# Laying x and the result out in token order of the tiles, and finishing the last four tiles from their first complete half

## The chip, the cores and the metric

The kernel runs on one core of one Trainium2 chip. The metric is the device time of one execution in microseconds. Beside it stands the profile of one execution: its span goes from the first to the last instruction.

The engines are named as in the profile: PE (TensorE, matmuls), PEld (its weight loads), DVE (VectorE), ACT (ScalarE), POOL (GpSimd), SP (SyncE). SP computes nothing here; it issues most of the loads and stores. A name with a q, such as SPq, is the sequencer of an engine, and rows of DMA issues stand there.

## The reference, cut to what matters

One layer of a hybrid encoder, in float32, over 1024 tokens of width 1024 and a feed-forward width of 2816:

```
h = x + 0.5 * swiglu(rms_norm(x, ffn1_norm), w_gate1, w_up1, w_down1)
h = h + merged_attention(rms_norm(h, mix_norm)) @ w_out
h = h + 0.5 * swiglu(rms_norm(h, ffn2_norm), w_gate2, w_up2, w_down2)
return rms_norm(h, final_norm)
```

with `rms_norm(x, g) = x * rsqrt(mean(x * x) + 1e-6) * g` for each token. The merged attention joins a two-dimensional neighbourhood attention (a grid of 16 rows of 64 columns) and a windowed attention through two gates. The change touches the first line's x and the last line's norm.

## The kernel before, in words

**Tiles.** The 1024 tokens are worked on as eight tiles of 128. A tile isn't 128 tokens in a row: because of the grid attention, tile b takes the eight columns 8b to 8b+7 of each of the 16 grid rows. A token is a row of 1024 floats, 4 KB. So in the arrays x and out, a tile is 16 groups of 8 rows; a group is 32 KB in one piece, and the groups lie 64 rows, 256 KB, apart. The views `x2` and `out2` (L41, L42) say this, and each load or store of a tile goes through them. What the kernel puts away for itself, such as the residual `h_d`, it lays out tile by tile, so that a tile is 128 rows in one piece.

**The residual** lives in eight tiles `res(t)`: 0 to 3 in the buffers `fx`, 4 to 7 in the four quarters of `fa`.

**Float32 products.** Each factor is split in a high and a low part (`split`, L88: ACT copies the high part, DVE subtracts; the rows L89 and L90 of the profile), and each product takes three matmuls (`mm3`, L138; L141, L143, L145). The large products use a Strassen-like scheme of seven block products with the names P1 to P7.

**The start.** `load_x` (L587) loads the eight x tiles in SP's queue: tile 0, then the gain of the norm, tiles 1 to 3, the first two blocks of weights, tiles 4 to 7, two more blocks of weights. `transition` (L160) takes the tiles through the norm (`normed`, L112), the transpose on PE (`turned`, L134) and `to_strassen` (L189), which splits them into right-hand factors and copies the transposed halves (L204, L205). The products of the first half feed-forward begin when the first four tiles are through. In `normed`, ACT squares a tile and sums the squares (L119), POOL turns the sum into a factor (L122, L123), and DVE scales (L125). Each engine works its instructions in the order of its own queue.

**The down projections** are made by the class `Down`. Its list `seq` holds 77 pairs of a block product and one of 11 blocks, in the order P2, P1, P5, P6, P3, P7, P4. `run` (L526) goes through all but the last five and prepares the factors up to seven entries ahead, in a ring of seven slots; a slot is free when PE is through with the entry that had it. `evict` (L518, the DVE rows at L523) adds a finished PSUM bank, times 0.5, to a half tile of the residual. P7 completes the high half (columns 512 to 1023) of tiles 4 to 7; P4 completes their low half and is the last product. The last five entries, all of P4, are done tile by tile: `tail(j)` (L545) multiplies them for tile 4+j and evicts that tile, so that the tiles end one after another. For the residual of the first half feed-forward x is loaded once more (L572, in `down_ffn`, L566); the second one loads `h_d` with the same line.

**The end.** The loop at L1186 runs the second half feed-forward's down projection. `finish` (L1180) takes tile t through the final norm in two halves and stores each half, 128 rows of 2 KB, through SP (L1184). Tiles 0 to 3 are finished while the P4 entries run; tiles 4 to 7 behind their `tail`. `normed` with `parts=2` squares both halves, and POOL adds the two sums (L121), adds EPS (L122) and raises to the power -0.5 (L123); then DVE scales both halves, and each is stored.

**Order.** Engines are synchronised by semaphores that a tile framework sets; it also places each engine's instructions, so the order on an engine can differ from that of the source. Buffers named xs, raw, ws come from pools of 2, 4 and 8; who takes a buffer waits until its last user is done, a store from it included.

Of the kernel before, what the change touches and what calls it, by code (L numbers as in the profile page):

```python
# [10 lines left out]
F32 = mybir.dt.float32  # L11
F32R = mybir.dt.float32r
AF = mybir.ActivationFunctionType
ALU = mybir.AluOpType

P = 128
T = 1024
D = 1024
NC8 = D // P
NTT = T // P  # L20
# [4 lines left out]
ROWS = T // GW  # L25
NEG = -1.0e30
BIG = 1.0e38
EPS = 1e-6
# [8 lines left out]
def trunk_kernel(ctx, tc, x, n1, wg1, wu1, wd1, nm, win, rpb, sink, wa, wb, wo,  # L37
                 n2, wg2, wu2, wd2, nf, c_rope, c_mask_a, c_mask_b, out):
    nc = tc.nc

    x2 = x.rearrange("o (r b w) d -> (o b) r w d", b=NTT, w=8)  # L41
    out2 = out.rearrange("o (r b w) d -> (o b) r w d", b=NTT, w=8)  # L42

    const = ctx.enter_context(tc.tile_pool(name="const", bufs=1))
    main = ctx.enter_context(tc.tile_pool(name="main", bufs=1))
# [5 lines left out]
    def nm_(s):  # L51
        uid[0] += 1
        return f"{s}_{uid[0]}"
# [3 lines left out]
    nhalf = const.tile([P, 1], F32, name="nhalf")  # L57
# [11 lines left out]
    def new_ar(g, dt=F32R):  # L69
        ar[g] = main.tile([P, 4, 1024], dt, tag=f"ar{g}", bufs=1, name=nm_("ar"))  # L70
        return ar[g]
# [7 lines left out]
    def raw4():  # L79
        return main.tile([P, 1024], F32, tag="raw", bufs=4, name=nm_("raw"))  # L80

    def xs4():
        return main.tile([P, 1024], F32, tag="xs", bufs=2, name=nm_("xs"))
# [23 lines left out]
    def load_gain(g):  # L107
        gb = const.tile([P, 1152], F32, tag="gain", bufs=1, name=nm_("gain"))
        nc.sync.dma_start(gb[:, :D], g.partition_broadcast(P))
        return gb[:, :D]  # L110

    def normed(h, gb, xs=None, parts=1):  # L112

        xs = xs4() if xs is None else xs
        w = D // parts
        cols = [slice(i * w, (i + 1) * w) for i in range(parts)]
        st = const.tile([P, 4], F32, tag="st", bufs=4, name=nm_("st"))
        for i, c in enumerate(cols):
            nc.scalar.activation(xs[:, c], h[:, c], AF.Square, scale=D ** -0.5, accum_out=st[:, i:i + 1])  # L119
        if parts == 2:  # L120
            nc.gpsimd.tensor_tensor(st[:, 0:1], st[:, 0:1], st[:, 1:2], op=ALU.add)  # L121
        nc.gpsimd.tensor_scalar(st[:, 0:1], st[:, 0:1], EPS, None, op0=ALU.add)  # L122
        nc.gpsimd.tensor_tensor(st[:, 2:3], st[:, 0:1], nhalf, op=ALU.pow)  # L123
        for c in cols:
            nc.vector.scalar_tensor_tensor(out=xs[:, c], in0=h[:, c], scalar=st[:, 2:3], in1=gb[:, c],  # L125
                                           op0=ALU.mult, op1=ALU.mult)
        return xs
# [25 lines left out]
    def res(t):  # L153

        return fx[t] if t < 4 else fa[:, (t - 4) * 1024:(t - 3) * 1024]
# [435 lines left out]
    gain = load_gain(n1[0])  # L591
# [22 lines left out]
    gain = load_gain(nm[0])  # L614
# [458 lines left out]
    for n in range(1 << 30):  # L1073
# [14 lines left out]
        if n in (59, 60, 61):  # L1088
            c = (59, 60, 61).index(n)
# [10 lines left out]
    t = new_ar(2, F32)  # L1100
# [42 lines left out]
    for i, dc in enumerate(a_order):  # L1143
        r = nxt.pop(0)
# [11 lines left out]
        for n in range(2):  # L1156
            sl = slice(n * 512, (n + 1) * 512)
# [6 lines left out]
    gain = load_gain(n2[0])  # L1164
# [13 lines left out]
    gain = load_gain(nf)  # L1178

    def finish(t):  # L1180
        y = normed(res(t), gain, raw4() if t in (5, 7) else None, 2)
        for n in range(2):
            sl = slice(n * 512, (n + 1) * 512)
            nc.sync.dma_start(out2[t][:, :, sl], y[:, sl])  # L1184

    for n, _ in enumerate(down.run()):  # L1186
        if n in (2, 5, 8, 11):
            finish(n // 3)
    for t in range(4, NTT):
        down.tail(t - 4)  # L1190
        finish(t)


def _consts():
# [53 lines left out]
```

## Time and profile before

| what | us |
|---|---|
| median of 3 runs | 1960.69 |
| lowest and highest run | 1960.07, 1963.54 |
| the profiled execution, its own time | 1959.04 |
| its span | 1956.9 |
| PE busy in the span | 1923.9 |
| DVE busy | 1432.2 |
| ACT busy | 951.6 |
| POOL busy | 337.1 |

How to read what is quoted below. The page of the profile begins with the busy time of each engine and with lines of 40 digits, one for each fortieth of the span: the busy share in tenths. The table by stretches has one row for each stretch, `from:to`, its length, and then for PE, PEld, DVE, ACT and POOL the busy time and, in brackets, the number of instructions; behind these stand the clock granted to PE, the mean busy share of the 16 DMA engines, and the GB/s they moved. In the rows in order of time stand start, duration, engine, line, operation, what is written and read, and the count; in square brackets the idle time of the engine just before, and what ended it. Rows of one line's instructions give the shortest, the median and the longest duration in ns, and the first and the last start in us. Rows of groups give the total busy time in us and the mean of one instruction in ns. The end of a matmul is modelled.

### The profile page before, as it was taken

The numbers are of one execution on the slowest core, as the hardware profiler recorded it, in microseconds if no ns is written. First come the engines' busy times: TensorE is split into PE (matmuls) and PEld (weight loads), VectorE is DVE, ScalarE is ACT, GpSimd is POOL, SyncE is SP. The second block draws the span as 40 slices with busy tenths as digits, with TensorE's granted clock in tenths as the row PEclk, the third lists the DMA queues.
The fourth block names the chain that finished last, engine by engine and source line by source line (L and its number), as shares of the span: only waits on it lengthen the run. The fifth ranks groups of instructions, "written<-read, shape, count | busy, mean of one in ns | idle before, by whom it ended". The sixth has DMA issues, their size and how long they took to land. (4 is left out here: it accounts for less than half of the span.)

```text
span 1956.9 us, 25669 instructions
## 1 busy us (share of the span) xinstructions
PE 1923.9 (98%) x8968; PEld 1603.6 (82%) x8968; DVE 1432.2 (73%) x2503; ACT 951.6 (49%) x1846; POOL 337.1 (17%) x469
## 2 busy tenths in 40 slices
PE   6999999999999999999999999999999999999997
PEld 5888888888888888888888888878888888888886
DVE  7976566557967688678888857989666566569864
ACT  7433333334446543467787873366333333344452
POOL 1010001002500112211112135510101001005110
PEclk9999999999999999999999999999999999999999
DMA  8433323369233558663359565544523323492341
GB/s 212 145 114 103 118 87 108 119 219 281 82 119 129 170 176 261 207 180 92 97 141 190 180 228 210 178 140 146 151 86 108 119 92 104 147 358 90 119 145 49
DMA packets 234784, 293.45 MB, mean 150 GB/s; under 512 B 14208, under 2 KB 161024, under 8 KB 234656
## 3 DMA queue, kind: packets, MB, share of 16 engines
q1 hardware_dynamic: 206816, 206.24, 34.7%
q0 software_dynamic: 27840, 85.58, 13.2%
q8 instruction: 71, 1.16, 0.2%
q14 instruction: 57, 0.47, 0.1%
HBM read 205.16 MB, written 86.70 MB: 149 GB/s over the span
## 5 line engine op out<-in xcount | busy, mean ns | idle before, releaser
L141 PE MATMUL g<-ar,ws 128*128 128x512 f32 x1152 | 432.9, 395 | 2.3 <-ACT ar L89 1.6
L143 PE MATMUL g<-ar,ws 128*128 128x512 f32 x1152 | 426.6, 390 | 0.0
L145 PE MATMUL g<-ar,ws 128*128 128x512 f32 x1152 | 425.4, 390 | 0.2 <-DVE ws L90 0.2
L90 DVE TENSOR_TENSOR ws<-raw,ws 128x512 fp32r<-128x512 f32 (+1 forms) x329 | 235.7, 722 | 176.9 <-ACT ws L89 175.6
L89 ACT CAST ws<-raw 128x512 fp32r<-128x512 f32 (+1 forms) x331 | 209.4, 638 | 289.3 <-PE g L145 123.0
L143 PE MATMUL d<-ar,ws 128*128 128x512 f32 x712 | 271.9, 389 | 1.1 <-POOL ar L90 1.1
L141 PE MATMUL d<-ar,ws 128*128 128x512 f32 x712 | 272.3, 390 | 0.6 <-ACT ws L89 0.5
L145 PE MATMUL d<-ar,ws 128*128 128x512 f32 x712 | 271.8, 389 | 0.6 <-DVE ws L90 0.5
L145 PEld LDWEIGHTS g<-ar,ws 128*128 128x128 f32 x1152 | 216.2, 188 | 46.5 <-DVE ws L90 0.7
L143 PEld LDWEIGHTS g<-ar,ws 128*128 128x128 f32 x1152 | 216.2, 188 | 45.5 <-DVE ar L90 0.3
L141 PEld LDWEIGHTS g<-ar,ws 128*128 128x128 f32 x1152 | 211.1, 188 | 40.8 <-ACT ar L89 2.0
L141 PEld LDWEIGHTS d<-ar,ws 128*128 128x128 f32 x712 | 133.6, 188 | 29.1 <-ACT ws L89 1.5
L143 PEld LDWEIGHTS d<-ar,ws 128*128 128x128 f32 x712 | 133.6, 188 | 29.0 <-POOL ar L90 1.5
L145 PEld LDWEIGHTS d<-ar,ws 128*128 128x128 f32 x712 | 133.6, 188 | 28.8 <-DVE ws L90 1.0
L356 POOL DMA_DIRECT2D hid<-fx x96 | 51.8, 540 | 504.1 <-DVE fx L398 380.3
L90 DVE TENSOR_TENSOR ws<-ar,ws 128x512 fp32r<-128x512 f32 x114 | 109.1, 964 | 5.0 <-ACT ws L89 5.0
L89 ACT CAST ar<-raw 128x512 fp32r<-128x512 f32 (+1 forms) x83 | 56.0, 678 | 91.5 <-PE g L143 53.1
L90 DVE TENSOR_TENSOR ws<-fa,ws 128x512 fp32r<-128x512 f32 x76 | 52.5, 691 | 53.3 <-ACT ws L89 52.9
L141 PE MATMUL g<-ws,ws 128*128 128x512 f32 x232 | 91.0, 392 | 0.0
L145 PE MATMUL g<-ws,ws 128*128 128x512 f32 x232 | 90.4, 390 | 0.0
L143 PE MATMUL g<-ws,ws 128*128 128x512 f32 x232 | 90.3, 389 | 0.0
L1021 ACT ACTIVATE fa<-fa,nmx 128x385 f32<-128x385 f32 (+3 forms) x128 | 75.5, 591 | 27.2 <-DVE nmx L1018 26.6
(234 smaller groups left out, 3508.0 us busy)
## 6 DMA issues: line engine op xcount, KB each, us to landing
raw<-hid SPq DMA_DIRECT2D x70, 512.0 KB
hid<-fx POOLq DMA_DIRECT2D x96, 256.0 KB, 2.5
raw<-in_ffn_w_up_dram SPq DMA_DIRECT2D x32, 512.0 KB
ar<-in_ffn_w_down_dram SPq DMA_DIRECT2D x32, 512.0 KB
raw<-in_ffn_w_gate_dram SPq DMA_DIRECT2D x28, 512.0 KB
hid<-fa POOLq DMA_DIRECT2D x54, 256.0 KB, 2.6
raw<-in_w_in_dram SPq DMA_DIRECT2D x27, 512.0 KB
ar<-zs_d POOLq DMA_DIRECT2D x48, 256.0 KB, 5.0
```

What stands on the lines that cost most here:

```text
L89: nc.scalar.copy(dst_hi, src)
L90: (eng or nc.vector).tensor_tensor(dst_lo, src, f32v(dst_hi), op=ALU.subtract)
L141: nc.tensor.matmul(b, lhs[0], r[0], start=first, stop=False, **kw)
L143: nc.tensor.matmul(b, lhs[0], r[1], start=False, stop=False, **kw)
L145: nc.tensor.matmul(b, lhs[1], r[0], start=False, stop=last, **kw)
L356: nc.gpsimd.dma_start(hid[PRODUCTS.index(p), i], src)
L1021: nc.scalar.activation(pr, pr, AF.Exp, scale=-1.0, bias=nmx[:, s:s + 1], accum_out=ssum[:, s:s + 1])
```

## The change

The host hands x over with the tokens sorted by tile, and puts the rows of the result back into token order when the kernel is done; neither is in the device time. The views `x2` and `out2` are then plain: a tile is 128 rows of 4 KB in one piece. All loads of x (L588, L572) and all stores of the result go through the new views.

The finish of tiles 4 to 7 is taken apart. When the P7 evictions have completed the high half, four calls of `begin`, one behind each of four P4 entries, square that half on ACT, add EPS to its sum on POOL, and multiply the half by the gain on DVE. Behind the tail of a tile, `rest` squares the low half on ACT, adds the two sums and raises to the power on POOL. `scale` multiplies the low half by factor and gain on DVE and stores it through SP, and multiplies the high half by the factor on ACT and stores it through ACT's own queue. In the source, `scale` of a tile stands behind the tail of the next one.

In the built program PE's instructions and their order are unchanged. On DVE, the eviction of tile 4 is followed by the low-half scaling of tile 4, then come the eviction of tile 5, the scaling of tile 5, and so on. On ACT, each of the last four tiles has the low square, the high scaling and the DMA issue one behind the other. The four squares and the four multiplications of `begin` stand between the casts and subtractions of the last factors.

```diff
-    x2 = x.rearrange("o (r b w) d -> (o b) r w d", b=NTT, w=8)
-    out2 = out.rearrange("o (r b w) d -> (o b) r w d", b=NTT, w=8)
+    x2 = x.rearrange("o (b p) d -> (o b) p d", p=P)
+    out2 = out.rearrange("o (b p) d -> (o b) p d", p=P)
...
-            nc.sync.dma_start(out2[t][:, :, sl], y[:, sl])
+            nc.sync.dma_start(out2[t][:, sl], y[:, sl])
+
+
+    LO, HI = slice(0, 512), slice(512, 1024)
+    late = {}
+
+    def square(t, c, k):
+        y, st = late[t]
+        nc.scalar.activation(y[:, c], res(t)[:, c], AF.Square, scale=D ** -0.5, accum_out=st[:, k:k + 1])
+
+    def begin(t):
+        y, st = late[t] = raw4() if t in (5, 7) else xs4(), const.tile([P, 4], F32, tag="st", bufs=4, name=nm_("st"))
+        square(t, HI, 1)
+        nc.gpsimd.tensor_scalar(st[:, 1:2], st[:, 1:2], EPS, None, op0=ALU.add)
+        nc.vector.tensor_tensor(y[:, HI], res(t)[:, HI], gain[:, HI], op=ALU.mult)
+
+    def rest(t):
+        square(t, LO, 0)
+        st = late[t][1]
+        nc.gpsimd.tensor_tensor(st[:, 0:1], st[:, 0:1], st[:, 1:2], op=ALU.add)
+        nc.gpsimd.tensor_tensor(st[:, 2:3], st[:, 0:1], nhalf, op=ALU.pow)
+
+    def scale(t):
+        y, st = late[t]
+        nc.vector.scalar_tensor_tensor(out=y[:, LO], in0=res(t)[:, LO], scalar=st[:, 2:3], in1=gain[:, LO],
+                                       op0=ALU.mult, op1=ALU.mult)
+        nc.sync.dma_start(out2[t][:, LO], y[:, LO])
+        nc.scalar.activation(y[:, HI], y[:, HI], AF.Copy, scale=st[:, 2:3])
+        nc.scalar.dma_start(out2[t][:, HI], y[:, HI])
 
     for n, _ in enumerate(down.run()):
         if n in (2, 5, 8, 11):
             finish(n // 3)
+        if n in (12, 13, 14, 15):
+            begin(n - 8)
     for t in range(4, NTT):
         down.tail(t - 4)
-        finish(t)
+        rest(t)
+        if t > 4:
+            scale(t - 1)
+    scale(NTT - 1)
...
     data.update(_consts())
+    order = np.arange(T).reshape(ROWS, NTT, 8).transpose(1, 0, 2).reshape(-1)
+    data["x"] = np.asarray(data["x"])[:, order]
...
-    return r.results[0]["out_0_dram"]
+    out = np.empty_like(r.results[0]["out_0_dram"])
+    out[:, order] = r.results[0]["out_0_dram"]
+    return out
```

## The prediction

> **What bounds the kernel now.** I read the page first, then a table by stretches of the span, then the instructions in order of time at both ends. The profiled execution took 1959.04 us, its span 1956.9; the sum is made in that span. The median of the runs shown is 1960.69, so 1.65 above it, and a gain found in the span is taken off 1960.69.
>
> ```profile
> span 1956.9 us, 25669 instructions
> ...
> PE 1923.9 (98%) x8968; PEld 1603.6 (82%) x8968; DVE 1432.2 (73%) x2503; ACT 951.6 (49%) x1846; POOL 337.1 (17%) x469
> ...
> PE   6999999999999999999999999999999999999997
> ```
>
> ```profile
> 24.40:30.00 5.60, 5.17 (x26) 4.23 (x27) 5.60 (x9) 5.38 (x11) 1.49 (x3) 1.00 1.14 272
> 30.00:40.00 10.00, 9.93 (x53) 8.05 (x51) 10.00 (x16) 9.87 (x19) 1.71 (x4) 1.00 0.76 188
> 40.00:60.00 20.00, 19.91 (x92) 16.34 (x92) 19.28 (x32) 12.37 (x23) 1.32 (x2) 1.00 0.48 159
> ...
> 1900.00:1946.90 46.90, 46.85 (x206) 38.17 (x204) 23.75 (x38) 17.18 (x36) 3.91 (x12) 1.00 0.24 71
> ```
>
> TensorE (second column) is busy from its first real matmul to its last, 0.6 us of gaps in the first 36 and almost none later; only the first and the last slice of the page are below 9. So the time is three pieces: the start up to that first matmul (24.41 us, row below), a body of 1922.5, and a tail from the last matmul's end (1946.48 + 0.39 = 1946.87) to 1956.9, 10.0 us. The change adds no matmul and moves none, so it can pay only at the two ends.
>
> **The start: x laid out in token order.** Eight x tiles are loaded by L588, four before the first weights.
>
> ```profile
> 5.82 1.06 ACT L119 ACTIVATE xs<-fx 128x1024 f32<-128x1024 f32 x1 [3.81 <-DMA fx<-in_x_dram]
> ...
> 10.03 1.06 ACT L119 ACTIVATE xs<-fx 128x1024 f32<-128x1024 f32 x1 [3.06 <-DMA fx<-in_x_dram]
> ...
> 14.15 1.06 ACT L119 ACTIVATE xs<-fx 128x1024 f32<-128x1024 f32 x1 [0.80 <-DMA fx<-in_x_dram]
> ...
> 16.15 0.63 ACT L89 CAST ws<-raw 128x512 fp32r<-128x512 f32 x1
> ...
> 18.32 0.59 ACT L204 COPY fx<-d 128x512 f32<-128x512 f32 x1 [0.56 <-DVE ar L90]
> ...
> 24.41 0.50 PE L141 MATMUL g<-ar,ws 128*128 128x512 f32 x1 [1.63 <-ACT ar L89]
> ```
>
> ACT waits for each of the first four x tiles. After the fourth (14.15) it is busy nearly without a break until it releases TensorE at 24.41. So the start moves with the landing of the fourth tile. How fast is such a load? The next rows are stretches in which little but one kind of load moves (the last two columns are DMA share and GB/s): x tiles in 8 to 12, then two loads of h_d in contiguous rows, then one load of the rope table, an input like x but contiguous.
>
> ```profile
> 8.00:12.00 4.00, 1.97 (x8) 1.57 (x8) 1.24 (x1) 1.15 (x2) 0.65 (x2) 1.00 1.04 241
> ...
> 1112.50:1114.50 2.00, 2.00 (x13) 1.74 (x12) 1.95 (x9) 1.93 (x6) 0.38 (x1) 1.00 0.93 373
> 703.40:705.00 1.60, 1.60 (x9) 1.33 (x8) 1.60 (x4) 1.60 (x5) 0.00 (x0) 1.00 0.84 310
> ...
> L572 SPq DMA_DIRECT2D fx<-in_x_dram x4: 536/557/612, 414.0 to 454.3; - x4
> ...
> L572 SPq DMA_DIRECT2D fx<-h_d x4: 332/335/339, 1702.6 to 1742.1; - x4
> ```
>
> The x load keeps the DMA engines fully busy (1.04) at 241 GB/s; the same 512 KB in contiguous rows moves at 373 (share 0.93). Both go in rows of 4 KB, so packet size is not it; what differs is where the 128 rows lie (16 groups of 8 rows, 256 KB apart, against one run). The rope row says that it is not that x is an input: 310 at a share of 0.84 is again about 370 at full share. After the change x has h_d's layout. A tile of 524 KB takes 524/241 = 2.17 us before and 1.41 at 373, 0.77 less. Of the first four tiles three come back to back at the slow rate (2.3 us saved). The first starts on an idle queue and should save about half as much (0.4), and its issue is 0.56 - 0.34 = 0.22 us shorter. That makes 2.9 us for the fourth tile. ACT's following chain needs the first weights (16.15, 2.0 us behind the fourth square) and these were loaded behind the x tiles, so they come earlier by as much; tiles 4 to 7 come earlier by more. **I take 2.9 us off the start.** Bounds: 0 if the layout is not the cause, 3.9 at the rate of 412 that the fastest contiguous stretch shows, with the first tile at full saving.
>
> ```profile
> 1743.50:1745.00 1.50, 1.50 (x8) 1.23 (x8) 1.11 (x2) 0.31 (x1) 0.00 (x0) 1.00 1.03 412
> ```
>
> (524/412 = 1.27 us, 0.90 less a tile, four tiles 3.6, and the shorter issue.) The residual loads of x (L572, four tiles to each half) run below a full TensorE and count for nothing.
>
> The Trainium skill bears on this, in "DMA: Bandwidth & Descriptors", section "Latency and other measured facts": copies whose rows lie a large power of two apart slow down, but at a pitch of 512 KiB by only 3% (207 against 214 GB/s), and much at 2 MiB. By that rule a jump of 256 KB costs almost nothing, and the start would gain an estimated 0.3 us (3% of four loads). This case's rows, 241 against 373, speak for more.
>
> **The tail: what each part costs.** Rows of the last two tiles, in order of time:
>
> ```profile
> 1936.70 0.69 DVE L523 SCALAR_TENSOR_TENSOR fa<-g,fa 128x512 f32<-128x512 f32 x1 [7.08 <-PE g L145]
> ...
> 1944.79 0.68 DVE L523 SCALAR_TENSOR_TENSOR fa<-g,fa 128x512 f32<-128x512 f32 x1
> ...
> 1946.48 0.39 PE L145 MATMUL g<-ar 128*128 128x512 f32 x1
> ...
> 1947.50 1.42 DVE L125 SCALAR_TENSOR_TENSOR xs<-fa,st,gain 128x512 f32<-128x512 f32 x2 [2.02 <-POOL st L123]
> ...
> 1948.83 0.68 DVE L523 SCALAR_TENSOR_TENSOR fa<-g,fa 128x512 f32<-128x512 f32 x1
> 1949.55 0.63 ACT L119 ACTIVATE raw<-fa 128x512 f32<-128x512 f32 x1 [2.70 <-DVE fa L523]
> ...
> 1950.34 0.19 POOL L121 TENSOR_TENSOR st<-st 128x1 f32<-128x1 f32 x1 [2.88 <-ACT raw L119]
> 1950.62 0.22 POOL L122 TENSOR_SCALAR st<-st 128x1 f32<-128x1 f32 x1
> 1950.93 0.57 POOL L123 TENSOR_TENSOR st<-st,nhalf 128x1 f32<-128x1 f32 x1
> 1951.53 1.42 DVE L125 SCALAR_TENSOR_TENSOR raw<-fa,st,gain 128x512 f32<-128x512 f32 x2 [2.02 <-POOL st L123]
> 1952.31 1.20 SPq L1184 DMA_DIRECT2D out_dram<-raw  x2
> ```
>
> Step 1, the evictions. TensorE releases the first of these evictions at 1936.70 and ends the fourth tile at 1946.87, so it needs 3.39 us for a tile, but VectorE evicts one every 4.04 (1944.79 to 1948.83), because each eviction stands behind both scalings of the tile before, and these behind the whole chain eviction, square, POOL, scaling. The last eviction comes at 1948.83, though its bank was full at 1946.87. The source wants the scaling of tile t-1 behind the eviction of t, but the built kernel still places scale t ahead of eviction t+1. What cures it is that the chain is shorter: eviction to square 0.72, square to POOL 0.79, add 0.28, power 0.60, one scaling instead of two 0.71: 3.1 us, under 3.39. So the last eviction starts at 1946.90: **1.93 us** gained.
>
> Step 2, POOL. Adding EPS (L122) is done ahead: 1950.93 - 1950.62 = **0.31 us**. The last scaling may start 2.70 - 0.31 = 2.39 us behind the eviction, at 1949.29 instead of 1951.53.
>
> Step 3, two halves on two engines. VectorE scales the low half (store on SP at 1949.29 + 0.78 = 1950.07), ACT the high half, already multiplied with the gain; nearest row a 128x512 ACTIVATE at 0.63, at most 0.75, its store from ACT at about 1950.0. Before, the second store was issued 0.66 behind the first. What that is worth depends on the transfers:
>
> ```profile
> 1953.00:1954.00 1.00, 0.00 (x0) 0.00 (x0) 0.00 (x0) 0.00 (x0) 0.00 (x0) 0.50 0.45 88
> 1954.00:1955.00 1.00, 0.00 (x0) 0.00 (x0) 0.00 (x0) 0.00 (x0) 0.00 (x0) 0.50 1.00 320
> 1955.00:1956.00 1.00, 0.00 (x0) 0.00 (x0) 0.00 (x0) 0.00 (x0) 0.00 (x0) 0.50 0.32 117
> ```
>
> The 525 KB flow from about 1953.55 to 1955.3 without a gap: the second store queues behind the first, so its earlier issue gains nothing by itself. The Trainium skill says the same in "DMA: Bandwidth & Descriptors", section "Issuing engines are not separate DMA queues": two issuers share the 16 DMA engines, and a second one saves only issue time. The trace agrees (share 1.00 at 320 GB/s); by that rule alone this step would give 0, by the issue times 0.66.
>
> Step 4, the layout of out. Here too 16 groups become one run: the issue was 0.54 us (next row) and should be about 0.34 as for h_d, and 320 GB/s may rise towards 373, 0.2 us over 525 KB. I take **0.4 us** for steps 3 and 4 together, with 0 and 0.9 as bounds.
>
> ```profile
> L1184 SPq DMA_DIRECT2D out_dram<-raw x4: 538/538/539, 1944.2 to 1953.0; - x4
> ```
>
> Sum of the tail: 1.93 + 0.31 + 0.4 = **2.6 us** (2.2 to 3.1); the wait for the last store and the end of the program stay as they are.
>
> **What is moved into the body.** Ahead of the last five blocks VectorE gets four multiplications of about 0.69 and ACT three squares of 0.8 (to the POOL step behind them, as above; the fourth stood ahead of the end already before).
>
> ```profile
> 1919.76 0.62 ACT L89 CAST ws<-raw 128x512 fp32r<-128x512 f32 x1 [1.39 <-PE g L145]
> ...
> 1925.62 0.69 DVE L90 TENSOR_TENSOR ar<-raw,ar 128x512 fp32r<-128x512 f32 x1 [1.43 <-ACT ar L89]
> ...
> 1937.43 0.63 ACT L119 ACTIVATE xs<-fa 128x512 f32<-128x512 f32 x1 [8.61 <-DVE fa L523]
> ...
> 1902.50 1.20 SPq L1184 DMA_DIRECT2D out_dram<-xs  x2
> ```
>
> There ACT idles 1.4 us before each pair of casts, waiting for TensorE to free a slot, and 8.6 us at the end; seven slots are ready ahead of TensorE. Cost nothing. Without that cover it would be 2.5 us of ACT. The new wait there is ACT's, for tile 3's store before it reuses its buffer; behind it stand the casts, for which TensorE would wait. That store is issued at 1902.50 (last row), and the square that reuses the buffer comes behind casts of about 1919, so it has long landed.
>
> ACT's DMA issue is new. SP's costs 0.54, POOL's 0.54:
>
> ```profile
> L356 POOL DMA_DIRECT2D hid<-fx x96 | 51.8, 540 | 504.1 <-DVE fx L398 380.3
> ...
> L588 SPq DMA_DIRECT2D fa<-in_x_dram x4: 597/598/6197, 7.7 to 15.2; - x4
> ```
>
> Behind it on ACT stands the square of the next tile. The high scaling of tile 6 ends near 1946.6, the issue near 1947.2, the last square is due at 1947.63: 0.4 us to spare, no cost. An issue of up to 6.2 us stands among the x loads of the start, where loads queue up; here the queue is empty. I take 0.54.
>
> **The rivals.**
> A. Forecast: 1960.69 - 2.9 - 2.6 = **1955.2**, own range 1953.1 (3.9 and 3.1 off, and 0.6 of scatter, the distance of the lowest run shown from the median) to 1956.9. Chance 0.70.
> B. The layout does not make the loads faster: the slow rate belongs to x's place in memory or to the crowd of loads at the start, not to the jumps. Then the start keeps the shorter issue alone (0.2) and the tail, without a faster transfer, 2.4: 1960.69 - 0.2 - 2.4 = 1958.1. For it: no row shows x itself in contiguous rows. Against: the rope row. Chance 0.15. The skill's rule on the row pitch, above, would lead to this time too.
> C. The x tiles come earlier but ACT or VectorE takes it back: VectorE and ACT are at 10.00 and 9.87 of 10 us between 30 and 40, and TensorE could start early and then wait. Of the start a third is left (1.0): 1957.1. Against: TensorE lost only 0.07 in those 10 us. Chance 0.09.
> D. Slower: ACT's issue takes as long as SP's worst. Each tile's ACT chain then lasts 0.8 + 0.9 + 0.7 + i, and the last square slips by 3 x (i - 1.0) us; with i = 6.2 that is 15.6 us, 1970.8. It outweighs the gains beyond the bound from i = 4.1 on. For it: the 6197 ns above. Against: the queue is empty between tiles. Chance 0.06.
>
> **How the numbers follow.** Within 0.2% (3.9 us, about what a measurement of this kernel can tell from no change) is 1956.8 to 1964.6: B, C's greater part. Faster: A and a little of C, 0.74; same 0.20; slower 0.06. The range, 1952.8 to 1958.4, takes in A, C and B with 0.3 beyond them on each side, and leaves out D and the scatter about B's upper end.
>
> **What would show it.** Start: the fourth square at about 11.2 instead of 14.15, first matmul near 21.5; x stretches at over 350 GB/s, x issues near 0.34 us. Tail: evictions 3.4 us apart, the last one 0.03 behind TensorE's end, the power 0.28 behind the add, ACT's and SP's stores issued within 0.1 us of each other, 7.4 us from the last matmul's end to the end of the span. Wrong would be: x still near 240 GB/s, ACT's issue over 1 us, or gaps in TensorE between 1915 and the last matmul.

## The result and the profile after

The changed kernel took 1955.76 us in the median of 17 runs, the kernel before 1960.81 in 17 runs beside them: a ratio of 0.9974 with a 95% interval of 0.9967 to 0.9982, 5.1 us faster (3.5 to 6.5). One of the 17 runs of the changed kernel took 2416 us at a granted clock of 0.75 and is left out of the ratio. The profiled execution took 1955.32 us, 3.7 less than the profiled one of before. The rest of the 5.1 lies in the executions: before's profile was 1.8 below the median of its runs, after's 0.4.

The page of the changed kernel:

```profile
span 1953.5 us, 25658 instructions
...
PE 1925.7 (99%) x8968; PEld 1605.1 (82%) x8968; DVE 1433.2 (73%) x2503; ACT 954.8 (49%) x1850; POOL 341.5 (17%) x469
...
PE   7999999999999999999999999999999999999998
```

TensorE has as many matmuls as before and is busy 1.8 us longer; the span is 3.4 shorter. Only the two end slices are below 9, as before. So the two ends again.

**The start.** ACT's and TensorE's instructions of the changed kernel in order of time show the squares of x tiles 0 and 3, the wait behind them and the first real matmul.

```profile
4.27 1.06 ACT L119 ACTIVATE xs<-fx 128x1024 f32<-128x1024 f32 x1 [2.27 <-DMA fx<-in_x_dram]
...
10.47 1.06 ACT L119 ACTIVATE xs<-fx 128x1024 f32<-128x1024 f32 x1 [0.24 <-DMA fx<-in_x_dram]
...
15.92 0.59 ACT L204 COPY fx<-d 128x512 f32<-128x512 f32 x1 [1.85 <-DVE ar L90]
...
22.01 0.80 PE L141 MATMUL g<-ar,ws 128*128 128x512 f32 x1 [1.62 <-ACT ar L89]
```

The first tile is 1.55 us earlier (5.82 before), the fourth 3.68 (14.15 before). The first matmul is only 2.40 earlier (24.41 before): 1.28 is lost between, and ACT's wait for VectorE ahead of L204, 0.56 before, is now 1.85, longer by just that. The stretch of the loads (the last two columns are DMA share and GB/s), and the times of the issues of x's first four tiles at L572 (shortest, median, longest in ns):

```profile
8.00:12.00 4.00, 2.64 (x12) 2.24 (x13) 1.34 (x2) 3.58 (x8) 2.31 (x5) 1.00 1.09 343
```

```profile
L572 SPq DMA_DIRECT2D fx<-in_x_dram x4: 341/346/489, 412.7 to 452.5; - x4
```

x now moves at 343 GB/s where it moved at 241, and such an issue in the quiet body takes 0.346 us instead of 0.557 in the median. What holds VectorE back shows in its rows and POOL's:

```profile
10.32 0.94 POOL L122 TENSOR_SCALAR st<-st 128x1 f32<-128x1 f32 x1 [0.46 <-ACT xs L119]
...
11.95 1.28 DVE L125 SCALAR_TENSOR_TENSOR xs<-fx,st,gain 128x1024 f32<-128x1024 f32 x1 [0.77 <-POOL st L123]
12.00 1.32 POOL L122 TENSOR_SCALAR st<-st 128x1 f32<-128x1 f32 x1
...
13.40 0.57 POOL L123 TENSOR_TENSOR st<-st,nhalf 128x1 f32<-128x1 f32 x1
14.00 1.28 DVE L125 SCALAR_TENSOR_TENSOR xs<-fx,st,gain 128x1024 f32<-128x1024 f32 x1 [0.77 <-POOL st L123]
```

POOL's addition of EPS to 128 numbers takes 0.22 us elsewhere. Here it takes 0.94 and 1.32, and ends 0.1 us behind the scaling that VectorE has under way (11.95 + 1.28 = 13.23; 12.00 + 1.32 = 13.32). So POOL makes the next factor only when VectorE is done with the last tile, and VectorE waits 0.77 for it: a tile each 2.05 us (11.95 to 14.00), though the tiles land 1.4 apart (9.08 and 10.47).

**Behind the first matmul.** TensorE in the changed kernel, then in the kernel before:

```profile
22.94 1.94 PE L134 MATMUL d<-ident,xs 128*128 128x128 f32 x8
...
25.10 0.63 PE L145 MATMUL g<-ar,ws 128*128 128x512 f32 x1
25.53 0.53 PE L141 MATMUL g<-ar,ws 128*128 128x512 f32 x1
25.89 0.39 PE L143 MATMUL g<-ar,ws 128*128 128x512 f32 x1
```

```profile
25.33 1.06 PE L134 MATMUL d<-ident,xs 128*128 128x128 f32 x8 [0.42 <-DVE xs L125]
26.15 0.47 PE L143 MATMUL g<-ar,ws 128*128 128x512 f32 x1
```

Until 25.5 the changed kernel's TensorE runs at half the pace that before's had: eight transposes in 1.94 us instead of 1.06, matmuls start 0.43 apart instead of 0.23. This isn't a mark of the change: with the old layout of x, the kernels of experiments 2, 3 and 6 below start their matmuls 0.43 apart too, up to 28.7, 30.7 and 29.1 us; the profiled execution of before happened to be without it. In the profiled pair the lead of 2.40 shrinks to 1.17 by then, and to 0.49 by the last matmul, in small steps in the attention and merge stages.

**The tail.** The last two evictions (L523) and the rest of the last tile:

```profile
1943.02 0.69 DVE L523 SCALAR_TENSOR_TENSOR fa<-g,fa 128x512 f32<-128x512 f32 x1 [0.27 <-PE g L145]
...
1945.99 0.39 PE L145 MATMUL g<-ar 128*128 128x512 f32 x1
...
1946.42 0.69 DVE L523 SCALAR_TENSOR_TENSOR fa<-g,fa 128x512 f32<-128x512 f32 x1 [0.27 <-PE g L145]
...
1948.22 0.55 POOL L1204 TENSOR_TENSOR st<-st,nhalf 128x1 f32<-128x1 f32 x1
1948.80 0.72 ACT L1211 ACTIVATE raw<-raw,st 128x512 f32<-128x512 f32 x1 [0.93 <-POOL st L1204]
1948.80 0.75 DVE L1208 SCALAR_TENSOR_TENSOR raw<-fa,st,gain 128x512 f32<-128x512 f32 x1 [1.69 <-POOL st L1204]
1949.55 0.37 ACTq L1212 DMA_DIRECT2D out_dram<-raw  x1
1949.58 0.33 SPq L1210 DMA_DIRECT2D out_dram<-raw  x1
```

The evictions are 3.4 us apart and wait for TensorE now (their idle time ends "<-PE"). The last one starts 0.04 behind the last matmul's end (1945.99 + 0.39), the two stores are issued 0.03 apart, and the span ends 7.1 us behind TensorE instead of 10.0.

### The profile page after: what moved, and what is told of

The parts are those of the page before. It is cut to its first block, busy times and chain, and to the rows that moved or that the text cites. A ratio compares the mean times of both kernels' runs of the same rounds, so it can differ in the third digit from the quotient of the medians.

```text
span 1953.5 us, 25658 instructions
## 1 busy us (share of the span) xinstructions
PE 1925.7 (99%) x8968; PEld 1605.1 (82%) x8968; DVE 1433.2 (73%) x2503; ACT 954.8 (49%) x1850; POOL 341.5 (17%) x469
## 4 chain that ended last, share of the span: by engine, by line
PE 86%; issue 6%; DVE 4%; POOL 2%; DMA 1%; ACT 1%; SPq 0%; POOLq 0%; ACTq 0%; DVEq 0%
PE g L141 16%; PE g L143 16%; PE g L145 16%; PE d L145 10%; PE d L143 10%; PE d L141 10%; PE d L1034 2%; PE d L1013 1%; PE d L1014 1%; PE g L1048 1%; PE g L1053 1%; DVE ws L90 1%; DVE ar L90 1%; PE d L134 1%; DVE ar L1159 1%
## 5 line engine op out<-in xcount | busy, mean ns | idle before, releaser
L90 DVE TENSOR_TENSOR ws<-raw,ws 128x512 fp32r<-128x512 f32 (+1 forms) x329 | 236.6, 724 | 175.4 <-ACT ws L89 174.1
L141 PEld LDWEIGHTS d<-ar,ws 128*128 128x128 f32 x712 | 133.6, 188 | 28.7 <-ACT ws L89 1.1
L90 DVE TENSOR_TENSOR ws<-ar,ws 128x512 fp32r<-128x512 f32 x114 | 110.2, 973 | 5.3 <-ACT ws L89 5.3
L90 DVE TENSOR_TENSOR ws<-fa,ws 128x512 fp32r<-128x512 f32 x76 | 52.5, 691 | 53.4 <-ACT ws L89 52.9
```

The lines of the kernel that those rows point to most:

```text
L90: (eng or nc.vector).tensor_tensor(dst_lo, src, f32v(dst_hi), op=ALU.subtract)
L141: nc.tensor.matmul(b, lhs[0], r[0], start=first, stop=False, **kw)
```

## The experiments

Each is timed beside the kernel before on its chip: 1962.15 us for the first four, 1962.12 for the next four, 1961.66 for the last four. The changed kernel itself ran beside the last four.

**1. The layout of x alone**, with the old finish and the old layout of the result; the diff is against the kernel before.

```diff
-    x2 = x.rearrange("o (r b w) d -> (o b) r w d", b=NTT, w=8)
+    x2 = x.rearrange("o (b p) d -> (o b) p d", p=P)
+    data["x"] = np.asarray(data["x"])[:, order]
```

> Only the load of x is laid out in token order of the tiles; the stores of the result keep their 16 groups and the finish is that of before. Theory (the contiguous x tiles load faster, and the start is worth what the profile after shows): x issues near 0.35 to 0.43 us, x stretches above 350 GB/s, first real matmul near 22.0 instead of 24.4, of which TensorE gives back some 1.2 us at half pace; the time falls by 1.2 to 2.4 us, to about 1958.5 to 1959.5 against 1960.8. Rival (the gain is all in the finish): within 0.5 us of before. Rival (the start is worth its 3.7 us of earlier loads in full): 1957.

1959.8 us, ratio 0.9987 (0.9979 to 0.9996), 2.4 us faster. The stretch from 8 to 12 us:

```profile
8.00:12.00 4.00, 2.64 (x12) 2.24 (x12) 1.46 (x2) 3.52 (x8) 2.39 (x5) 1.00 1.09 338
```

The start has its gain by itself, and the rate belongs to the layout of x, not to x being an input.

**2. The old groups at another distance.** The kernel before, with a grid row of x padded by one token, so that the 16 groups of a tile lie 260 KB apart instead of 256. Again against the kernel before:

```diff
-    x2 = x.rearrange("o (r b w) d -> (o b) r w d", b=NTT, w=8)
+    x2 = x.rearrange("o (r g) d -> o r g d", g=65)[0, :, :64, :].rearrange("r (b w) d -> b r w d", w=8)
```

> x keeps its 16 groups of 8 rows to a tile, but the host pads each grid row of 64 tokens by one token, so that the groups lie 260 KB apart instead of 256; all else as before. Theory A (the jump by a power of two slows the load, since it sends the 16 DMA engines to the same place of the memory): 4 KB rows come at the pace of contiguous ones, over 340 GB/s between 8 and 12 us at full DMA share, and the start moves as with x laid out contiguously, 1 to 2.4 us. Theory B (groups as such are slow, whatever their distance): 240 GB/s as before, no change of time. In both the issue stays near 0.55 us, since its form is that of before.

1962.18 us, ratio 1.0000 (0.9992 to 1.0009). The same stretch:

```profile
8.00:12.00 4.00, 1.97 (x8) 1.56 (x8) 1.28 (x1) 1.15 (x2) 1.07 (x3) 1.00 1.04 242
```

Nothing moved. The power of two in the distance was not the cause, so the Trainium skill's rule on the row pitch ("DMA: Bandwidth & Descriptors", section "Latency and other measured facts"), weighed in the prediction, does not bear on these loads.

**3. The finish alone**, with both old layouts.

```diff
-    x2 = x.rearrange("o (b p) d -> (o b) p d", p=P)
-    out2 = out.rearrange("o (b p) d -> (o b) p d", p=P)
+    x2 = x.rearrange("o (r b w) d -> (o b) r w d", b=NTT, w=8)
+    out2 = out.rearrange("o (r b w) d -> (o b) r w d", b=NTT, w=8)
```

> Only the new finish of the last four tiles, with ACT's store queue; x and the result keep their 16 groups. Theory (the tail gains by the shorter chain, not by the layout): evictions 3.4 us apart, from the last matmul's end to the end of the span 7.4 to 7.8 us instead of 10.0, time 2.2 to 2.6 us below before, 1958.3. Rival (the layout of the stores carries a good part of the 2.9 us seen): under 1.8 us. The start stays at 24.4.

1959.26 us, ratio 0.9989 (0.9980 to 0.9998), 2.9 us faster. With the first experiment's 2.4 that is about the whole gain: as far as these intervals can tell, the two parts add up. Its last matmul and its stores (span 1959.6):

```profile
1951.44 0.39 PE L145 MATMUL g<-ar 128*128 128x512 f32 x1
...
1954.99 0.55 ACTq L1212 DMA_DIRECT2D out_dram<-raw  x1
1955.02 0.54 SPq L1210 DMA_DIRECT2D out_dram<-raw  x1
```

The tail is 1959.6 - 1951.83 = 7.8 us, 0.65 longer than with the new layout of the result (7.1).

**4. One queue.** The whole change, with the high half stored through SP as well.

```diff
-        nc.scalar.dma_start(out2[t][:, HI], y[:, HI])
+        nc.sync.dma_start(out2[t][:, HI], y[:, HI])
```

> The whole change, but the high half is stored through SP too. Theory (the two stores share the same DMA engines, so a second queue saves at most the second issue): the last issue comes 0.37 us later, the end 0 to 0.4 us later than with two queues, 1955.8 to 1956.2. Rival (two queues move the last 512 KB faster): the last transfer takes over 0.5 us longer and the time is over 0.6 us above that of the whole change.

1955.84 us, ratio 0.9964 (0.9951 to 0.9978). Its tail (span 1954.0):

```profile
1946.73 0.39 PE L145 MATMUL g<-ar 128*128 128x512 f32 x1
...
1950.28 0.33 SPq L1212 DMA_DIRECT2D out_dram<-raw  x1
1950.71 0.38 SPq L1210 DMA_DIRECT2D out_dram<-raw  x1
```

From the last matmul's end to the span's end are 6.9 us, no more than with two queues. From the first of the two stores' issue to the end: 4.6 us before (1952.31 to 1956.9), 4.6 with two queues and the old layout, 3.95 with two queues and the new, 3.7 with one queue and the new. The layout makes the difference, the second queue none.

**5 and 6. What about the layout of x slows it?** Two kernels hold the whole change but another x. In the fifth, the 128 rows of a tile lie singly, 32 KB apart, as one even list. In the sixth they are again 16 groups of 8, with one row left out between groups, so that all lie within 572 KB.

```diff
-    x2 = x.rearrange("o (b p) d -> (o b) p d", p=P)
+    x2 = x.rearrange("o (p b) d -> (o b) p d", b=NTT)
```

```diff
-    x2 = x.rearrange("o (b p) d -> (o b) p d", p=P)
+    x2 = x.rearrange("o (b r g) d -> (o b) r g d", r=16, g=9)[:, :, :8, :]
```

> The whole change, but x laid out so that the 128 rows of a tile lie one by one, 32 KB apart, at one even pitch: no two rows of a tile touch, and the transfer is one list of 128 rows instead of 16 groups of 8. Theory (the form of the access, 16 groups, is what slows the loads; where the rows lie is not): as fast as in the changed kernel, 8 to 12 us at 340 GB/s or more, x issues near 0.4 us, first matmul near 22.0, time 1955.8 (1954.8 to 1957). Rival (rows that don't lie next to each other in memory load slowly): 8 to 12 us at 240 GB/s or less, issues near 0.6, fourth square near 14.2, first matmul 24.4, time 1958.3.

> The whole change, but a tile of x consists again of 16 groups of 8 rows, now with only one row (4 KB) left out between groups, so that the tile covers 572 KB instead of 4 MB. Theory (16 groups in the access slow the load, however close they lie): 8 to 12 us at about 240 GB/s, x issues near 0.6 us, first matmul near 24.4, time about 1958.3 (the tail's gain is kept). Rival (distance in memory decides): 340 GB/s or more, issues near 0.4, first matmul near 22.0, time 1955.8.

Single rows far apart: 1957.56 us, ratio 0.9978 (0.9969 to 0.9987). Groups close together: 1958.94 us, ratio 0.9979 (0.9970 to 0.9989). The stretch from 8 to 12 us in the one and in the other:

```profile
8.00:12.00 4.00, 1.97 (x8) 1.57 (x8) 1.60 (x2) 2.93 (x5) 1.54 (x3) 1.00 1.08 356
```

```profile
8.00:12.00 4.00, 1.97 (x8) 1.57 (x8) 1.28 (x1) 1.15 (x2) 0.76 (x2) 1.00 1.05 240
```

The ratios of the two are alike; it is the traces that tell them apart, with first matmuls at 22.95 (rows apart) and 25.16 us (groups close). It is the form: 16 groups in the access are slow even where they almost touch, and 128 single rows are fast even 32 KB apart. Distance has a small price of its own: in the fifth kernel the first square comes at 4.77 and the second at 8.70 instead of 4.27 and 7.75, the first matmul 0.94 later than in the changed kernel, and its time misses the expected range by 0.6 us. Why 16 groups are slow stays open. The Trainium skill, "DMA: Bandwidth & Descriptors", section "Why a DMA increments its semaphore by 16 and not by 1", says that the slowest dimension of an access decides over how many DMA engines it is spread; 16 groups would still be spread over 16, so that rule alone does not give the loss (241 GB/s against 343).

**7. The gain in PSUM.** If VectorE's scaling holds up POOL, a scaling with only one input in SBUF should not. The gain is copied to two PSUM banks, and tiles 1 to 3 are scaled from there in halves.

```diff
+                early.extend(bank("g") for _ in range(2))
+                for k in range(2):
+                    nc.vector.tensor_copy(early[1 + k], gb[:, k * 512:(k + 1) * 512])
...
-            nc.vector.scalar_tensor_tensor(out=xs[:, c], in0=h[:, c], scalar=st[:, 2:3], in1=gb[:, c],
+            nc.vector.scalar_tensor_tensor(out=xs[:, c], in0=h[:, c], scalar=st[:, 2:3], in1=g,
```

> The whole change, but VectorE's scalings of x tiles 1 to 3 take the gain from two banks of PSUM (copied there once), in halves, so that these operations have one input in SBUF instead of two. Theory (POOL's 128x1 addition took 0.94 and 1.32 us instead of 0.22 since VectorE's scaling with two inputs in SBUF held it up): all additions of the start near 0.22 us, the last of the four scalings ends 0.5 to 1 us earlier than the 15.2 of the changed kernel; if ACT's chain follows, the first matmul comes at 21.0 to 21.6 and the time is 1954.9 to 1955.6. Rival (the addition is late for another reason, such as the crowd of transfers): it still takes 0.9 and 1.3 us, time 1955.8 or up to 0.5 more, since the scaling in halves costs 0.1 us each and the two copies 1.3 us before the first scaling.

1954.35 us, ratio 0.9963 (0.9950 to 0.9975). VectorE, POOL and the first matmul:

```profile
9.83 2.77 DVE L142 SCALAR_TENSOR_TENSOR xs<-fx,st,g 128x512 f32<-128x512 f32 x4 [0.98 <-POOL st L125]
```

```profile
10.29 0.22 POOL L124 TENSOR_SCALAR st<-st 128x1 f32<-128x1 f32 x1 [0.49 <-ACT xs L121]
...
11.61 0.22 POOL L124 TENSOR_SCALAR st<-st 128x1 f32<-128x1 f32 x1 [0.45 <-ACT xs L121]
```

```profile
19.44 0.50 PE L158 MATMUL g<-ar,ws 128*128 128x512 f32 x1 [1.74 <-ACT ar L89]
```

POOL's additions are back at 0.22 us beside a running scaling, and two tiles' scalings follow each other without a gap. The first matmul is 2.6 us earlier than in the changed kernel, more than the 1 us expected, since the built order changed as well: VectorE now subtracts for tile 0 ahead of tile 3's scaling, and ACT's wait ahead of the copies is gone.

**11. The halves without PSUM**, to tell these apart: the same halves, the gain in SBUF.

```diff
-            gs = early[1:3]
+            gs = [gb[:, c] for c in cols]
```

> The whole change, with VectorE's scalings of x tiles 1 to 3 in halves as in the kernel with the gain in PSUM, but with the gain in SBUF. Theory (the gain in PSUM earned its time by freeing POOL): POOL's additions still take over 0.6 us where a scaling is under way, the scaling of tile 3 starts later than the 13.2 at which it could there, first matmul at 21.2 to 22.2, time as the changed kernel or up to 0.7 us less. Rival (only the halves and the order of VectorE's work that follows from them made the gain): first matmul near 19.5, time 1.5 us below the changed kernel.

1956.61 us, ratio 0.9975 (0.9966 to 0.9983), no faster than the changed kernel beside it (1955.99). POOL, with its additions (L124) and powers (L125), and the first matmul:

```profile
10.81 0.92 POOL L125 TENSOR_TENSOR st<-st,nhalf 128x1 f32<-128x1 f32 x1
11.82 0.78 POOL L124 TENSOR_SCALAR st<-st 128x1 f32<-128x1 f32 x1
12.68 0.92 POOL L125 TENSOR_TENSOR st<-st,nhalf 128x1 f32<-128x1 f32 x1
```

```profile
20.93 0.79 PE L154 MATMUL g<-ar,ws 128*128 128x512 f32 x1 [1.59 <-ACT ar L89]
```

POOL is held up again, now the power too (0.92 instead of 0.57). So VectorE's second input in SBUF is what holds it. This is the rule of the Trainium skill, "SBUF — State Buffer", section "SBUF: two separate sides": VectorE with two inputs in SBUF and GpSimd reading SBUF shut each other out for a whole instruction; these rows agree, as far as POOL waiting for VectorE goes. The halves alone bring the first matmul 1.1 us forward, of which the time shows nothing; where that went was not followed up. The order on VectorE isn't that of experiment 7 either: there the first subtractions for tile 0 (L90, at 12.52) stand ahead of both halves of tile 3's scaling, here behind the first half (13.64 and 14.31). So the two experiments show what holds POOL up, but how much of the 1.5 us between their first matmuls (19.44 and 20.93) is POOL's and how much the order's is not shown.

**8. TensorE kept busy in the start.** 25 more transposes of x tiles, whose results nobody reads.

```diff
+    spins = {0: 5, 1: 13, 3: 7}
...
+        spin = spins.pop(t, 0)
+        for i in range(0, spin, 4):
+            pt = bank("g")
+            for c in range(min(4, spin - i)):
+                nc.tensor.transpose(pt[:, c * P:(c + 1) * P], xs[:, c * P:(c + 1) * P], ident)
```

> The whole change, with 25 transposes of x tiles more on TensorE (5 behind tile 0's, 13 behind tile 1's, 7 among tile 3's), whose results nobody reads, so that TensorE has little idle time between 10 and 22 us. Theory (TensorE runs at half pace for some us behind the first matmul, 128x512 in 0.63 instead of 0.39 and a transpose in 0.24, since it was idle before; this takes back part of what the earlier loads gain, more or less from run to run): matmuls take 0.39 to 0.40 from the first on, eight transposes 1.06 us instead of 1.94, time 1954.0 to 1955.0, if the extra transposes don't delay the real ones. Rival (the pace has nothing to do with the idle time; or the extra work delays tile 3's transposes): 0.63 still, first matmul at 22.0 to 23.0, time 1955.8 to 1957.

1956.38 us, ratio 0.9970 (0.9958 to 0.9981): no gain, though the first matmul comes 1.2 us earlier (20.80 against 22.01). TensorE:

```profile
20.80 0.51 PE L141 MATMUL g<-ar,ws 128*128 128x512 f32 x1 [0.69 <-ACT ar L89]
22.37 0.81 PE L134 MATMUL d<-ident,xs 128*128 128x128 f32 x4 [1.06 <-ACT fx L211]
...
23.54 0.63 PE L145 MATMUL g<-ar,ws 128*128 128x512 f32 x1
```

The extra work came in the wrong place: two idle stretches of 0.69 and 1.06 us stayed close ahead of the half pace. It could not decide.

**9 and 12. The same in the right place.** The kernel with the gain in PSUM, once more as it is (12), and with 17 extra transposes, 5 behind tile 1's and 12 behind the last ones of tile 3 (9). The instructions of VectorE and ACT stand in the same order in both.

The diff is against the kernel with the gain in PSUM; the loop is that of experiment 8, here over the second half of a tile's columns.

```diff
+    spins = {1: 5, 3: 12}
```

> The kernel with the gain in PSUM once more, beside the changed kernel on one chip. If its first matmul 2.6 us earlier is kept to the end: 2 to 2.6 us below the changed kernel; if the half pace behind it and the stages of the body give a part back, as for the change itself: 1.0 to 1.8 us below.

> The kernel with the gain in PSUM, with 17 transposes more on TensorE whose results nobody reads: 5 behind tile 1's, 12 behind tile 3's, so that the stretch of 1.74 us before the first matmul (17.70 to 19.44 in that kernel) is filled. Theory (TensorE's pace in a stretch of about 3.4 us is set by whether it was idle in the stretch before): the half pace between 20.4 and 24.5 is gone or shorter, first matmuls at 0.39 to 0.40, time 0.5 to 1.5 us below the kernel without them. Rival (the remaining 0.46 us of idle time before tile 4's transposes is enough for the half pace, or the pace doesn't depend on idle time): 0.63 us a matmul for 3 us as before, time the same or, with the extra transposes at half pace in front of the first matmul, up to 1.2 us more.

The changed kernel on this chip (10):

> The changed kernel itself, as the mark for the other three on this chip: 1955 to 1957 us, 0.9974 of the kernel before.

| kernel | median us | range (runs) | ratio to before |
|---|---|---|---|
| changed kernel (10) | 1955.99 | 1955.07 to 1957.55 (8) | 0.9972 (0.9962 to 0.9982) |
| gain in PSUM (12) | 1954.22 | 1952.82 to 1955.23 (5) | 0.9962 (0.9948 to 0.9975) |
| and 17 transposes (9) | 1953.04 | 1952.56 to 1953.86 (5) | 0.9957 (0.9945 to 0.9970) |

TensorE with the gain in PSUM (12), two stretches of it by the table (the first column behind the length is PE's busy time, the one behind POOL's the clock), and then TensorE with the 17 transposes (9) and a stretch of that:

```profile
21.77 0.63 PE L162 MATMUL g<-ar,ws 128*128 128x512 f32 x1
22.20 0.63 PE L158 MATMUL g<-ar,ws 128*128 128x512 f32 x1
```

```profile
17.77:21.18 3.41, 1.31 (x9) 1.04 (x10) 2.64 (x4) 3.41 (x9) 1.05 (x3) 1.00 1.12 303
21.18:24.59 3.41, 3.41 (x11) 2.73 (x10) 3.41 (x6) 3.39 (x7) 0.57 (x2) 0.50 1.17 294
```

```profile
19.45 0.50 PE L158 MATMUL g<-ar,ws 128*128 128x512 f32 x1 [1.02 <-ACT ar L89]
20.41 1.06 PE L151 MATMUL d<-ident,xs 128*128 128x128 f32 x8 [0.46 <-DVE xs L142]
21.23 0.48 PE L160 MATMUL g<-ar,ws 128*128 128x512 f32 x1
21.55 0.40 PE L162 MATMUL g<-ar,ws 128*128 128x512 f32 x1
```

```profile
18.63:22.04 3.41, 2.13 (x13) 1.71 (x14) 3.06 (x5) 3.40 (x7) 1.11 (x3) 1.00 1.17 291
```

The first matmul is at the same time in both (19.39 and 19.45). Without the extra transposes TensorE idles 1.74 us ahead of it and then runs at a clock of 0.50 from 21.18 to 24.59; with them it idles 1.02 and does not slow down. The kernel with the extra, useless work has a median 1.2 us lower, but with five runs each and ranges that overlap this is not clear of the scatter. It is the fastest version in the median: 8.6 us below the kernel before, and its five runs lie below all eight of the changed kernel. The Trainium skill, "TensorE: Matmul & The Clock Gate", section "What's actually happening", gives the mechanism: the clock is set by the activity in a free-running window of about 3.4 us. The trace agrees in the half clock (matmuls 0.43 apart instead of 0.23) and in the length of the slow stretch, 3.41 us. In the 3.41 us ahead of it TensorE was busy for 1.31.

That the extra transposes are what kept the clock up in 9 is not shown. The trace's records of the clock put the windows elsewhere in each execution. In 9, counted in steps of 3.41 us from its first record at 11.80, one of them is 18.63 to 22.04, the last row above, busy for 2.13. The twelve transposes behind tile 3's end before it, at 18.42, so this window would hardly have been idler without them. What speaks for them is an estimate from the two traces: wherever a window of 3.41 us is laid between 12 and 22 us, TensorE is busy in it for at least 1.80 us with the extra work, and for as little as 1.20 without. Half clock followed on 1.01 to 1.63 at the start of seven traces (1, 4, 5, 7, 8, 10, 12); windows with 1.80 or more kept the full clock (1.80 in before, 23.22 to 26.63). Where between them the limit lies these runs don't tell; near the end of the program 1.58 and 1.62 kept it too.

## Why the prediction was right, point by point

It forecast 1955.2; the median came 0.6 above it, inside its own range. Both ends gained, the body gave nothing, and the mechanism at each end was the one named, except for one step. That the start's sum came close all the same is luck in part: a landing that gained more than forecast hid most of a loss behind it.

**The layout makes the loads faster: right.** The argument from contiguous rows of other loads (373 GB/s against 241) held: 343 GB/s in the crowd, and x alone shows it (experiment 1). "What differs is where the 128 rows lie" was the wrong half of the sentence: the form of the access decides, not the place (2, 5, 6). For this change both come to the same.

**2.9 us for the fourth tile: mis-sized.** It was 3.68. The three tiles behind the first came 0.71 each, against 0.77 taken. The first was the miss: 0.62 taken (0.4 and the issue), 1.55 measured. Its issue gave 0.29 of that (0.68 before, 0.39 now); why the transfer gave the rest, where half of a tile's saving was assumed, was not followed up.

**"So the start moves with the landing of the fourth tile": this step failed.** The chain behind the fourth square was taken as fixed. It grew by 1.28 us, since tiles that land 1.4 us apart meet VectorE and POOL, of which VectorE's scaling holds POOL up, so that the pair needs 2.05 a tile (7, 11). Before, the tiles came 2.1 apart and the pair just kept up; faster loads made it the bound. The sign stood in the profile before: the 0.56 us for which ACT waits for VectorE ahead of L204, a row that the prediction shows and reads as "busy nearly without a break". That is rival C's mechanism (the gain is taken back by an engine of the start), with VectorE and POOL as the place. It took 1.28 of 3.68, not the two thirds that the rival had priced.

**TensorE's pace: not foreseen, and not a price of the change.** The half pace behind the first matmul comes with either layout of x; before's profile happened to have none. So the profiled pair keeps 1.17 us of the start's gain at 25.5 us and 0.49 at the last matmul, while the medians keep about 2.2 (5.1 less the tail's 2.9), near the 2.40 by which the first matmul is earlier. Against the 2.9 taken, the landing gave 0.78 more (3.68) and the chain behind it took 1.28 back. The small steps between 25.5 us and the last matmul were not taken apart.

**The tail: 2.6 taken, 2.9 measured.** Step 1 (evictions) gave 1.92 against 1.93; the last eviction waited 1.96 before (1948.83 less 1946.87) and 0.04 now. Step 2 held: the last scaling starts 2.38 us behind its eviction, 2.39 was forecast. Steps 3 and 4 had 0.4 together and gave 0.65 to 0.7: all of it from the layout of the result (3 against the changed kernel), nothing from the second queue (4). That agrees with the Trainium skill's rule in "DMA: Bandwidth & Descriptors", section "Issuing engines are not separate DMA queues", as the prediction gave it.

**What was moved into the body: right.** TensorE is busy 31.28 of the 31.30 us from 1915 to its end.

```profile
1915.00:1946.30 31.30, 31.28 (x138) 25.34 (x136) 15.96 (x25) 12.63 (x27) 3.88 (x10) 1.00 0.09 34
```

**The rivals.** B (the layout does not matter) fell with experiment 1. D (a long issue on ACT) fell at once: 0.37 us. C came in part.

## What to carry to other kernels

Look at how an access is cut up, not only at how far apart its rows lie: here 16 groups of 8 rows loaded at 241 GB/s, and 128 even rows at 338 to 356, with a shorter issue as well. When a transfer that sets the pace is made faster, price the stage behind it at the new pace; a pair of engines that just kept up may be the next bound. An idle stretch of TensorE can cost a second time behind it: here 1.74 us of waiting ahead of the matmuls stood before 3.41 us at half clock. Whether filling such a stretch pays has to be seen over many executions; five of each were too few.

## What the runs showed of the hardware that was not expected

- VectorE with two SBUF inputs holds POOL up for its whole length: a 128x1 addition of 0.22 us took up to 1.32, a power 0.92 instead of 0.57. With one of the inputs in PSUM, POOL's addition ran beside it in 0.22.
- The clock column of the profile does not show every half clock. It showed 0.50 in the kernel with the gain in PSUM from 21.18 to 24.59, but 1.00 throughout in the changed kernel, whose matmuls took the same 0.63 us up to 25.5. The trace's records of the clock say why: the changed kernel's first record begins at 25.81 us, where its matmuls come to full pace, and where there is no record the column reads 1.00. The pace was half from the first transposes on (eight in 1.97 us). The times of equal matmuls are the safer witness.
- Rows of 4 KB at 32 KB distance load as fast as contiguous ones once the stream runs (356 GB/s); only the first tile came 0.5 us later and the second 0.95, and those behind kept about that distance (the fourth 0.9).
